# A small first load, one 8 KB run per DMA engine, ahead of a queue of 6 MB loads

## The chip, the cores and the metric

The kernel runs on one core of a Trainium2 chip. The metric is device time of one execution in microseconds (us), median of several runs; lower is better. "Before" and "after" are the two kernels of the change. The profiled run of before took 335.77 us for a span of 334.0 us: the span starts at the program's first instruction on the core, and the time is some 1.8 us longer than the span.

## The reference

Adaptive max pooling of a float32 tensor of 32 x 256 x 4096 down to 256 outputs per row. As 4096 / 256 = 16, it is the maximum of each run of 16 neighbouring elements:

```python
for i in range(output_size):                      # 256
    start = int(i * length / output_size)         # 16 * i
    end = int((i + 1) * length / output_size)
    result[:, :, i] = np.max(x[:, :, start:end], axis=-1)
```

134.2 MB go in, 8.4 MB go out, and every input element is read once.

## The kernel before

The output is seen as 2,097,152 windows in a row. Two groups of windows are dealt to the 128 partitions (rows) of the on-chip memory, 7600 and 8784 windows each. A load brings 760 windows (48,640 B) to every partition, 6080 KB in all; the ring has three slots, so load n waits for the reduction of load n-3. VectorE reduces each slot into an output tile that stays on the chip, and the three stores stand at the end of the same queue.

```python
    SLOTS = 3
    CHUNK = 760
    GROUPS = [10 * CHUNK, total - 10 * CHUNK]     # total = 16384
    CUT = 10 * CHUNK
    ...
    for g, n in enumerate(GROUPS):
        xg = xw[first : first + P * n].rearrange("(p n) w -> p (n w)", p=P)
        ...
        for a in range(0, n, CHUNK):
            b = min(a + CHUNK, n)
            slot = ring[:, n_loads % SLOTS, 0 : (b - a) * W]
            n_loads += 1
            nc.sync.dma_start(out=slot, in_=xg[:, a * W : b * W])
            nc.vector.reduce_max(
                out=outs[g][:, a:b],
                in_=slot.rearrange("p (n w) -> p n w", w=W),
                axis=mybir.AxisListType.X,
            )
        ...                                        # note the stores of the group
    for dst, src in stores:
        nc.sync.dma_start(out=dst, in_=src)
```

That makes 22 loads (21 of 760 windows, a last one of 424) and 3 stores, 25 DMAs on one queue.

## Time and profile before

335.86 us, median of 6 runs (335.66 to 336.07). These are the lines of the page of before: the span, busy time, the slices (40 equal ones, DMA in tenths of the engines' time), the queue and the costliest group (busy us, mean ns of one, idle time before it and what ended it).

```profile
span 334.0 us, 111 instructions
DVE 276.3 (83%) x22; POOL 0.2 (0%) x4
DMA  9999899999999999999998999999999999989997
q1 hardware_dynamic: 3600, 142.61, 99.1%
L59 DVE TENSOR_REDUCE out<-ring 128x760 f32<-128x12160 f32 (+1 forms) x22 | 276.3, 12565 | 49.2 <-DMA ring<-in_x_dram 49.2
```

The DMA engines work all the time (99.1% of the span); VectorE waits only for loads. The timeline of before at its start (start us, us, engine and line, operation) shows the pace:

```profile
0.73 59.20 SPq L58 DMA_DIRECT2D ring<-in_x_dram  x6
18.01 12.82 DVE L59 TENSOR_REDUCE out<-ring 128x760 f32<-128x12160 f32 x1 [18.01 <-DMA ring<-in_x_dram]
32.38 12.82 DVE L59 TENSOR_REDUCE out<-ring 128x760 f32<-128x12160 f32 x1 [1.55 <-DMA ring<-in_x_dram]
46.76 12.82 DVE L59 TENSOR_REDUCE out<-ring 128x760 f32<-128x12160 f32 x1 [1.56 <-DMA ring<-in_x_dram]
```

A load every 14.38 us is 433 GB/s, and a reduction is 1.56 us shorter. Only head and tail are left to gain: the first reduction starts at 18.01 us, 3.6 us later than one load lasts.

The head needs a finer view. The trace holds a record of every DMA packet (one row of one load) and of every raise of a DMA's semaphore, the counter that the program waits for: 400 raises for the 25 DMAs of before, 16 each. No record names the engine; the 16 packets that start together are taken to be one of each engine, and so are the 16 raises of a DMA, called completions below. In the table below, and in all like it, times are us after the first load's issue, and they are read from those records. A row of 48,640 B takes 1.80 us in the steady state (1.796 to 1.81); the first ones do not:

```
                         first packets of 16 engines:  start          took          median
before                                                 1.01 to 2.44   1.79 to 3.09  2.53
first load complete on the earliest / mean / latest engine: 16.31 / 16.67 / 17.26
last store complete on the earliest / latest engine: 331.54 / 332.48
```

The spread of 0.95 us between the engines arises in the first row and is still 0.93 us at the end; over all 25 DMAs it is 0.92 to 0.96 us. The rows behind the first take 1.796 to 1.81 us on all engines, so none catches up, and the kernel ends with its latest engine.

### The profile page before, as it was taken

The page shows a single profiled execution, that of the slowest core. Times are in us where ns is not written, and L with a number is a line of the kernel's source. Part 1 is how long each engine was busy: PE and PEld are TensorE (multiplying, and loading weights), DVE is VectorE, ACT ScalarE, POOL GpSimd, SP SyncE. Part 2 cuts the span into 40 slices and gives each one's busy share as a digit, 9 for nine tenths or more (in the row PEclk, how much of TensorE's full clock was granted, in tenths as well). Part 3 has the DMA queues.
Part 4 walks back from the last instruction along what each step waited for, and adds up shares of the span by engine and source line. Part 5 has one row for each costly group of instructions (what it writes and reads, how often), then busy time and mean ns, then how long its engine had stood idle before and what let it go on. Part 6 is the DMA issues. An engine that isn't in the chain of part 4 may idle for free.

```text
span 334.0 us, 111 instructions
## 1 busy us (share of the span) xinstructions
DVE 276.3 (83%) x22; POOL 0.2 (0%) x4
## 2 busy tenths in 40 slices
DVE  0088989889898988989898898988989898898990
POOL 0000000000000000000000000000000000000000
DMA  9999899999999999999998999999999999989997
GB/s 361 390 460 454 384 466 437 402 466 437 402 460 425 419 454 408 443 454 396 454 454 384 466 437 402 466 419 419 460 414 431 454 408 443 454 384 440 443 419 306
DMA packets 3600, 142.61 MB, mean 427 GB/s; under 512 B 400, under 2 KB 400, under 8 KB 528
## 3 DMA queue, kind: packets, MB, share of 16 engines
q1 hardware_dynamic: 3600, 142.61, 99.1%
HBM read 134.22 MB, written 8.39 MB: 427 GB/s over the span
## 4 chain that ended last, share of the span: by engine, by line
DMA 68%; DVE 27%; DVEq 2%; SPq 0%; issue 0%
DMA ring<-in_x_dram 68%; DVE out L59 27%; DVEq L102 2%; SPq L58 0%
## 5 line engine op out<-in xcount | busy, mean ns | idle before, releaser
L59 DVE TENSOR_REDUCE out<-ring 128x760 f32<-128x12160 f32 (+1 forms) x22 | 276.3, 12565 | 49.2 <-DMA ring<-in_x_dram 49.2
L88 POOL MEMSET const-bfloat16-1.0<- 128x1 bf16 x1 | 0.1, 101 | 0.0
L88 POOL MEMSET const-uint8-127<- 128x1 uint8 x1 | 0.1, 101 | 0.0
L88 POOL MEMSET const-float32-0.0<- 128x1 f32 x1 | 0.1, 98 | 0.2 <-issue 0.2
L88 POOL MEMSET const-float32-1.0<- 128x1 f32 x1 | 0.1, 98 | 0.0
## 6 DMA issues: line engine op xcount, KB each, us to landing
ring<-in_x_dram SPq DMA_DIRECT2D x21, 6080.0 KB, 30.3
out_dram<-out SPq DMA_DIRECT2D x2, 3800.0 KB, 30.1
ring<-in_x_dram SPq DMA_DIRECT2D x1, 3392.0 KB, 23.9
out_dram<-out SPq DMA_DIRECT2D x1, 592.0 KB, 7.6
```

What stands on the lines that cost most here:

```text
L59: nc.vector.reduce_max(out=outs[g][:, a:b], in_=slot.rearrange("p (n w) -> p n w", w=W), axis=mybir.AxisListType.X,)
L88: nc = _bacc.Bacc("TRN2", target_bir_lowering=False, num_devices=1)
L102: with _tile.TileContext(nc) as tc:
```

## The change

The intent is to let the start of the DMA engines fall on a small load: 16 partitions with 8 KB each, meant as one run for each of the 16 engines, at the head of the queue. The remaining windows are dealt to 128 partitions as before, so the last load shrinks from 424 to 408 windows; the small load has its own reduction and its own store, second among the stores.

```diff
-    GROUPS = [10 * CHUNK, total - 10 * CHUNK]
+    FIRST_P, FIRST = 16, 128
+    rest = (total - FIRST_P * FIRST) // P
+    GROUPS = [10 * CHUNK, rest - 10 * CHUNK]
...
+    xf, of = group(FIRST_P, FIRST)
+    first_out = pool.tile([FIRST_P, FIRST], fp32, tag="first", name="first")
+    slot = next_slot(FIRST_P, FIRST)          # ring[0:16, 0, 0:2048]
+    nc.sync.dma_start(out=slot, in_=xf)
+    pooled(first_out, slot)
...
+    stores.insert(1, (of, first_out))
```

The rest of the diff puts loading, slots and reductions into small helpers and changes nothing that runs.

More of the change, by code (lines that the diff above doesn't have):

```diff
@@ L28 @@
     W = L // O
-    total = B * C * O // P
+    total = B * C * O
     SLOTS = 3
     CHUNK = 760
-    GROUPS = [10 * CHUNK, total - 10 * CHUNK]
+    FIRST_P, FIRST = 16, 128
+    rest = (total - FIRST_P * FIRST) // P
+    GROUPS = [10 * CHUNK, rest - 10 * CHUNK]
     CUT = 10 * CHUNK
-    assert sum(GROUPS) == total and B * C * O % P == 0
     pool = ctx.enter_context(tc.tile_pool(name="pool", bufs=1))
     ring = pool.tile([P, SLOTS, CHUNK * W], fp32, tag="ring", name="ring")
-    outs = [
-        pool.tile([P, n], fp32, tag=f"out{i}", name=f"out{i}")
-        for i, n in enumerate(GROUPS)
-    ]
@@ L44, with group, next_slot @@
     xw = x.flatten_outer_dims().rearrange("r (o w) -> (r o) w", w=W)
     ow = out.flatten_outer_dims().rearrange("r o -> (r o)")
+    taken = 0
+    def group(parts, n):
+        nonlocal taken
+        span = slice(taken, taken + parts * n)
+        taken += parts * n
+        return (
+            xw[span].rearrange("(p n) w -> p (n w)", p=parts),
+            ow[span].rearrange("(p n) -> p n", p=parts),
+        )
+    n_loads = 0
+    def next_slot(parts, n):
+        nonlocal n_loads
+        slot = ring[0:parts, n_loads % SLOTS, 0 : n * W]
+        n_loads += 1
+        return slot
@@ new lines, in pooled, with load @@
+    def pooled(dst, src):
+        nc.vector.reduce_max(
+            out=dst,
+            in_=src.rearrange("p (n w) -> p n w", w=W),
+            axis=mybir.AxisListType.X,
+        )
+    def load(dst, src, a, b):
+        slot = next_slot(P, b - a)
+        nc.sync.dma_start(out=slot, in_=src[:, a * W : b * W])
+        pooled(dst[:, a:b], slot)
+    xf, of = group(FIRST_P, FIRST)
+    first_out = pool.tile([FIRST_P, FIRST], fp32, tag="first", name="first")
+    slot = next_slot(FIRST_P, FIRST)
@@ L47 @@
+    nc.sync.dma_start(out=slot, in_=xf)
+    pooled(first_out, slot)
     stores = []
-    n_loads = 0
-    first = 0
     for g, n in enumerate(GROUPS):
-        xg = xw[first : first + P * n].rearrange("(p n) w -> p (n w)", p=P)
-        og = ow[first : first + P * n].rearrange("(p n) -> p n", p=P)
-        first += P * n
+        xg, og = group(P, n)
+        o = pool.tile([P, n], fp32, tag=f"out{g}", name=f"out{g}")
         for a in range(0, n, CHUNK):
-            b = min(a + CHUNK, n)
-            slot = ring[:, n_loads % SLOTS, 0 : (b - a) * W]
-            n_loads += 1
-            nc.sync.dma_start(out=slot, in_=xg[:, a * W : b * W])
-            nc.vector.reduce_max(
-                out=outs[g][:, a:b],
-                in_=slot.rearrange("p (n w) -> p n w", w=W),
-                axis=mybir.AxisListType.X,
-            )
-        if g < len(GROUPS) - 1:
-            stores.append((og, outs[g]))
-        else:
-            for a, b in ((0, CUT), (CUT, n)):
-                stores.append((og[:, a:b], outs[g][:, a:b]))
+            load(o, xg, a, min(a + CHUNK, n))
+        for a, b in ((0, CUT), (CUT, n)):
+            if a < b:
+                stores.append((og[:, a:b], o[:, a:b]))
@@ L70 @@
+    assert taken == total
+    stores.insert(1, (of, first_out))
     for dst, src in stores:
```

## The prediction

> **What bounds the kernel now.** The DMA engines, all the way. The page has DMA at 9 tenths in nearly every slice, mean 427 GB/s; VectorE is busy 83%. The chain of waits repeats every three loads, after 43.1 us: one 6080 KB load costs 14.38 us, 433 GB/s.[...] A reduction takes 12.82 us, 1.56 us less than a load, and the queue never runs dry. The three stores run at the same rate behind the last load. Bytes alone, 142.6 MB at 433 GB/s, are 329.4 us of the 334.0 us span. What is left, about 4.6 us, is head and tail.
>
> **The head.** By the trace's records of DMA packets (a 48,640 B row is one packet), the first issue begins at 0.73 us, the first packets start at 1.74 us, and an engine's first packet takes 2.3 to 3.1 us, where every later one takes 1.796 us. The 16 engines end their first packets between 4.13 and 5.08 us: a stagger of 0.95 us. As all engines then run at one rate and none starves, the stagger is kept to the end: the last store's completions are spread over 0.93 us too. The kernel ends with its latest engine.
>
> **What the change does.** It puts a 128 KB load ahead, one 8 KB run for each of 16 engines ([...]no view of this profile names the engine), so that the start latency falls on a small packet and all engines join together. Total bytes are the same: the last load shrinks from 424 to 408 windows, 8 KB less per engine. Three large loads stay outstanding, as before.
>
> **Costs.** One more load completion, about 0.03 us (14.376 less 8 x 1.793)[...]. Together 0.1 us. The added reduction is 2048 elements deep, estimated 12.82 x 2048/12160 = 2.2 us, while VectorE idles until 18 us: free. The added issue on the sync queue, 0.33 to 0.43 us, is hidden: the 8 KB packet needs 0.3 us at rate plus the latency, and the next load's rows should be there by then.
>
> **Gain.** The first read's latency stays. Only the stagger can go[...]. The most to gain is some 0.6 to 0.9 us; I expect about half, 0.45 us, less the 0.1 us of costs.
>
> **Prediction.** 335.5 us, range 334.9 to 336.1. Faster by over 2%: 0.005; within 2%: 0.985; slower: 0.01.
>
> **What would show it.** Packet records: starts of the first large packets and their spread under 0.95 us (right), or unchanged (no gain). The first 760-window reduction then begins at about 18.0 us or less plus the 0.3 us of the 8 KB packet. The period of 14.38 us and the reductions' 12.82 us stay.
>
> **What would make it wrong.** A hole between the small load and the first large one[...]; a small load that meets as much stagger as a large one; a shift of addresses (the second group's rows are now 548 KB apart, not 549 KB) that changes what HBM delivers.

The forecast's sum is before's 335.86 us, less 0.45 us expected of the stagger, plus 0.1 us of costs: 335.5 us. Only the 0.03 us of a completion are worked out from the trace, so the 0.1 us, like the 0.45 us, are estimates. That the small load gives each engine one run is inferred: in the trace of after, 16 packets of 8 KB start 1.03 to 1.21 us after the issue and take 0.49 to 0.52 us.

## The result, and the profile after

After: 335.88 us, median of 6 runs (335.73 to 336.04), against 335.86 us. The ratio is 1.0001, with a 95% interval of 0.9988 to 1.0014. Ratios here are the mean time of one kernel's fast runs over that of the other's of the same rounds, so not quite the ratio of the medians quoted.

The page of after, the same lines as of before:

```profile
span 334.1 us, 115 instructions
DVE 278.4 (83%) x23; POOL 0.2 (0%) x4
DMA  7998998999999999999989989999999999899997
q1 hardware_dynamic: 3664, 142.61, 99.1%
L67 DVE TENSOR_REDUCE out<-ring 128x760 f32<-128x12160 f32 (+1 forms) x22 | 276.1, 12553 | 43.6 <-DMA ring<-in_x_dram 43.6
L67 DVE TENSOR_REDUCE first<-ring 16x128 f32<-16x2048 f32 x1 | 2.3, 2274 | 3.7 <-DMA ring<-in_x_dram 3.7
```

The timeline of after at its start:

```profile
0.73 0.39 SPq L81 DMA_DIRECT2D ring<-in_x_dram  x1
1.18 59.04 SPq L75 DMA_DIRECT2D ring<-in_x_dram  x6
3.66 2.27 DVE L67 TENSOR_REDUCE first<-ring 16x128 f32<-16x2048 f32 x1 [3.66 <-DMA ring<-in_x_dram]
18.28 12.82 DVE L67 TENSOR_REDUCE out<-ring 128x760 f32<-128x12160 f32 x1 [12.34 <-DMA ring<-in_x_dram]
32.66 12.82 DVE L67 TENSOR_REDUCE out<-ring 128x760 f32<-128x12160 f32 x1 [1.56 <-DMA ring<-in_x_dram]
```

The added reduction lies in time in which VectorE has nothing else to do, the period is 14.38 us as before, and the first large load is reduced 0.27 us later. The small load's 8 KB per engine are worth 0.30 us at the steady rate (8192 / 48,640 x 1.793; 1.793 us is the commonest distance from one row's start to the next on an engine), so almost nothing was gained. The records of packets and completions, with a second trace of each kernel (first experiment below):

```
                 first full load, less bytes ahead       last store   sync's drain after
                 earliest  mean    latest    spread      (latest)     the last completion   span
before           16.31     16.67   17.26     0.95        332.48       0.062                 334.00
before, again    16.32     16.66   17.37     1.05        332.58       0.063                 334.11
after            16.69     16.88   17.22     0.53        332.40       0.194                 334.06
after, again     16.59     16.81   17.25     0.67        332.43       0.194                 334.08
```

"Less bytes ahead" means that the 0.30 us of the small load are taken off; "spread" is the latest engine less the earliest; the drain is the instruction of the sync queue behind its last wait. The stagger did shrink, from about 1.0 to 0.6 us. But it shrank because the earliest engines became 0.3 us later; the latest engine, which alone counts, gained less than 0.1 us on average. The last store completes 0.11 us earlier, and the program's end takes 0.13 us longer. Together that is 0.02 us more, the same as the difference of the medians; as one head differs from the next by more than that (before_27 below), so close an agreement is luck.

So there are three questions. Why does the large load behind the small one not start at full rate? Why did the spread shrink all the same? And where do the 0.13 us at the end come from?

### The profile page after: what moved, and what is told of

Same layout as the page of the kernel before. It is cut to its first block, busy times and chain, and to the rows that moved or that the text cites. A ratio compares the mean times of both kernels' runs of the same rounds, so it can differ in the third digit from the quotient of the medians.

```text
span 334.1 us, 115 instructions
## 1 busy us (share of the span) xinstructions
DVE 278.4 (83%) x23; POOL 0.2 (0%) x4
## 3 DMA queue, kind: packets, MB, share of 16 engines
q1 hardware_dynamic: 3664, 142.61, 99.1%
## 4 chain that ended last, share of the span: by engine, by line
DMA 68%; DVE 28%; DVEq 2%; issue 0%
DMA ring<-in_x_dram 68%; DVE out L67 27%; DVEq L128 2%; DVE first L67 1%
## 5 line engine op out<-in xcount | busy, mean ns | idle before, releaser
L67 DVE TENSOR_REDUCE first<-ring 16x128 f32<-16x2048 f32 x1 | 2.3, 2274 | 3.7 <-DMA ring<-in_x_dram 3.7
```

Of the source, the lines that this page charges most:

```text
L67: nc.vector.reduce_max(out=dst, in_=src.rearrange("p (n w) -> p n w", w=W), axis=mybir.AxisListType.X,)
```

## The experiments

Twelve runs were made, two of them repeats and ten of new kernels, on chips 0, 11, 12 and 13. Every ratio is taken against before in the same rounds (its medians were 335.96, 335.85, 335.86 and 335.79 us); the packet tables set traces of different chips side by side. At first there were three theories. **Delivery**: the rows of a 128-row load reach the last engine late, 2.4 us after the issue. **Placement** ("ports" in the texts): a load to 16 neighbouring partitions, as the small one to partitions 0 to 15, takes longer per byte than one to all 128. It was an assumption, to be tested; no view shows a port, and the "4ports" and "16ports" of three labels are names only, for partitions 0 to 15 and for every fourth one from 32 to 92. **First burst**: the first large reads are slow whatever ran before. A fourth came up on the way, **cover**: short rows start cheaply, and enough of them ahead cover the start of the long ones. All four are guesses until a run below shows them.

### before_again and after_again: is the stagger the program's?

Edit: none.

> The kernel before once more, for its packet records: is the head's stagger a property of the program or of one run? All theories of the program: latest completion of the first load again near 17.26 us after the first issue, spread over the engines near 0.95 us, one engine starting some 2.4 us after the issue. If the stagger is chance, spread and latest engine move by several tenths of a us.

> The changed kernel once more. If the head belongs to the program: latest completion of the first large load near 17.52 us after the first issue (0.27 us later than before, of which 0.30 us are the 8 KB ahead), spread near 0.53 us. If it is chance, both move by several tenths.

Measured: 335.89 and 335.86 us (one run each; state unknown, as for any single run), and the lines of the table above. In these two pairs the head belongs to the program, within about 0.1 us (a third trace of before's head, in before_27 below, is 0.3 us off). The late starter does not: no engine of before_again started later than 1.71 us after the issue, while one of before started at 2.44 us.

### split8_step and split8_block: eight loads of 16 rows in place of the first load

```diff
-            nc.sync.dma_start(out=slot, in_=xg[:, a * W : b * W])
+            if n_loads == 1:
+                for j in range(8):
+                    rows = slice(j, P, 8)                # split8_step
+                    rows = slice(16 * j, 16 * j + 16)    # split8_block
+                    nc.sync.dma_start(out=slot[rows], in_=xg[rows, a * W : b * W])
+            else:
+                nc.sync.dma_start(out=slot, in_=xg[:, a * W : b * W])
```

> The kernel before, with its first load cut into eight loads of 16 rows each (rows j, j+8, j+16 ...), so every engine gets one row per load; no small load, no further store. Theory delivery (the rows of a 128-row load reach the last engine only 2.4 us after its issue): every engine has its first row about 1.0 us after the issue, no late starter, latest completion of the first load 0.5 to 1 us earlier than before's 17.26, less 7 x 0.03 us of completions: about 16.7; time about 335.3. Theory first burst (16 large first reads together are slow, whoever issues them): first packets again 2.3 to 3.1 us, latest completion at 17.3 to 17.5, time about 336.1.[...]

> As split8_step, but each of the eight loads takes 16 neighbouring partitions, as the small load of the change does. Theory ports[...]:[...] time up to +43 us, and packets of up to 7 us in the head.[...] Theories delivery and first burst without ports: as split8_step within 0.2 us.

(The +43 us and the 7 us are estimates. Measured were +38.5 us over before and 6.72 us for a load.)

Measured: split8_step 351.14 us (ratio 1.0453, 1.0439 to 1.0467), split8_block 374.42 us (1.1143, 1.1128 to 1.1158). The first reduction, which needs all eight loads, in the timelines of split8_step and of split8_block:

```profile
33.68 12.82 DVE L64 TENSOR_REDUCE out<-ring 128x760 f32<-128x12160 f32 x1 [33.68 <-DMA ring<-in_x_dram]
```

```profile
56.97 12.82 DVE L64 TENSOR_REDUCE out<-ring 128x760 f32<-128x12160 f32 x1 [56.97 <-DMA ring<-in_x_dram]
```

And the GB/s of the slices on the page of split8_block, where the first six slices (9.3 us each) are the eight small loads:

```profile
GB/s 167 84 120 131 84 162 423 418 418 418 433 470 433 418 418 418 470 449 418 418 418 433 470 433 418 418 423 470 444 418 418 418 438 470 428 418 419 438 424 326
```

One 760 KB load over 16 neighbouring partitions took 6.72 us, so 778,240 B / 6.72 us = 116 GB/s; over partitions 8 apart 3.79 us, 205 GB/s; a load over all 128 runs at 433 GB/s. The pages have the DMA engines busy 7 to 9 tenths of those first six slices in split8_block and 8 to 9 tenths of the first four in split8_step, so idle engines are not what limits these loads.

What follows: a load to 16 neighbouring partitions had about a quarter of the rate of a load to all 128 (116 of 433 GB/s). By what mechanism, the traces do not show. An estimate from the 116 GB/s: the small load's 131,072 B take 1.13 us, not the 0.30 us that I had counted. These two kernels cannot tell delivery from first burst, since the slow placement swamps both.

### dead_small_4ports and dead_small_16ports: does the placement eat the gain at 8 KB?

A load that nothing reads is put at the head of the kernel before, into slot 2 of the ring:

```diff
+    dead = ring[0:16, 2, 0:2048]        # dead_small_4ports
+    dead = ring[32:96:4, 2, 0:2048]     # dead_small_16ports
+    nc.sync.dma_start(
+        out=dead, in_=xw[0 : 16 * 2048 // W].rearrange("(p n) w -> p (n w)", p=16)
+    )
```

> The kernel before with one more load at the head, 8 KB into each of partitions 0 to 15, of data that nothing reads: the change's head alone, without its reduction, its store and its shorter last load. Bytes: 0.30 us more than before. All theories: the head of the changed kernel comes back, latest completion of the first large load 17.5 us after the first issue (before: 17.26 and 17.37 in two traces; after: 17.52 and 17.55), engines spread 0.5 to 0.7 us. Time about 336.2.

> The same, into partitions 32, 36, ... 92[...]. Theory ports[...]: latest completion of the first large load falls below that of the 4-port run by 0.3 us or more, to 17.2 or less; time about 335.9. Theories delivery and first burst: within 0.1 us of the 4-port run.

(That loads to every fourth partition are written faster than loads to 16 neighbours was assumed here.)

Measured: 336.25 us (ratio 1.0014, 1.0001 to 1.0026) and 336.80 us (1.0027, 1.0014 to 1.0039).

```
                      first full load, less 0.30      8 KB packets    first 16 rows of 48,640 B
                      earliest  mean   latest spread  took            start         took (median)
dead_small_4ports     16.71     16.87  17.24  0.53    0.52            1.54 to 2.83  2.49
dead_small_16ports    16.83     17.25  18.04  1.21    0.35 to 0.56    1.81 to 2.67  2.50
```

dead_small_4ports reproduces after's head to 0.02 us, so reduction, store and sizes have no part in it. dead_small_16ports was expected to be better by 0.3 us or more if the placement ate the gain, and within 0.1 us otherwise; it is worse by 0.8 us, which no theory had. It is not a clean comparison: its packets started 1.34 us after the issue, not 1.01, and the next issue came 0.63 us after the first instead of 0.44, both seemingly a cost of the strided partitions. But taking off 0.34 us still leaves 17.70. So the placement does not eat the gain at this size. What stands out is the spread: 0.53 us on partitions 0 to 15, 1.21 us on every fourth one.

### dead_row_16ports: a whole row per engine ahead

```diff
-    dead = ring[32:96:4, 2, 0:2048]
+    dead = ring[32:96:4, 2, 0:12160]
```

with the source cut to match.

> [...]a whole row of 48,640 B per engine, 1.79 us of work each. Theory delivery (the last engine's rows of the 128-row load come 2.4 us after its own issue, 2.9 us after the first): every engine is busy with its one row until 3.3 us, so no engine starts the large load late; latest completion of the first large load 18.3 to 18.5, spread 0.3 us or less; time about 337.0, 0.8 us less than its bytes (before + 1.82 = 337.7). Theory first burst (16 large rows at once take 0.5 to 1.3 us longer, and once only): the same delay falls on the dead row and stays, latest completion 19.1 to 19.2, time about 337.7. If the large load meets the burst a second time, more than 19.2.

(The partitions are those of dead_small_16ports, 32 to 92 in steps of four.)

Measured: 337.79 us (ratio 1.0060, 1.0046 to 1.0073); latest completion of the first full load 19.15 us, spread 0.70 us. Eleven engines started their dead row 1.36 to 1.72 us after the issue, five of them at 2.21 to 2.31 us, although only one row per engine had to be delivered. So a late first start is not the delivery of 128 rows, and theory delivery falls. Less its 1.79 us of bytes this load is at 17.36 us, by the number the "first burst" figure; less the 0.34 us of the strided form, which the expectation had not allowed for, it is at 17.02, between the two. It does not settle first burst.

### before_27: is the end's 0.13 us a matter of counting?

```diff
-            stores.append((og, outs[g]))
+            for a, b in ((0, 2560), (2560, 5120), (5120, n)):
+                stores.append((og[:, a:b], outs[g][:, a:b]))
```

> The kernel before with its first store in three parts, 27 DMAs as in the changed kernel, the head untouched. In the traces of after, the sync queue waits at the end for the last store's semaphore first, and three finished ones are still to be waited for: its drain begins 0.194 us after the last completion, against 0.062 us before. If that comes of the count of DMAs alone (eight semaphores in turn), it shows here as well: 0.19 us. Two further completions cost 2 x 0.03 us in the stores. Time about 336.1, 0.2 us over before. If the end's wait comes of the small load or its store: 0.06 us and about 335.95.

Measured: 336.37 us (ratio 1.0013, 1.0001 to 1.0026). The drain begins 0.195 us after the last completion, as in after. The dead-load kernels with 26 DMAs have 0.126 and 0.127 us, before with 25 has 0.062. In the traces of before and after, the DMAs take eight semaphores in turn (48 or 64 raises on each), and the sync queue waits for them at the end in the same order of four pairs, 65 to 70 ns from one wait that is met to the next. With 25 DMAs (before) the last store's semaphore is in the last pair, with 27 (after) in the second (not the first, as the expectation has it), and so, by the turn, with 26 in the third; the later waits follow although they have long been met. So the change's 0.13 us come of having two DMAs more, not of what they do. The two added stores, which also have shorter rows (10,240 B against 30,400), cost 0.15 us between the last load and the last store (19.70 against 19.55 us), more than the 0.06 us expected of two completions. In the profiled run the rest came from the head, which is before's own program: its latest engine was at 17.63 us this time. So the latest engine of before has 17.26, 17.37 and 17.63 us in three traces, and a difference of 0.2 us in the time of one kernel is chance.

### first_256: 16 KB per engine instead of 8 KB

```diff
-    FIRST_P, FIRST = 16, 128
+    FIRST_P, FIRST = 16, 256
```

> The changed kernel with a first run of 16 KB per engine in place of 8 KB (the last load shrinks by as much). [...] Two theories are left for why the large load behind the 8 KB pays its own start. Theory cover (8 KB are gone 0.3 to 0.5 us after they start, before the large load's first reads are answered; a longer run covers more of them): latest completion of the first large load, less the bytes ahead (0.60 us), 17.0 or less, where the changed kernel has 17.22 and 17.25; time about 335.6. Theory first burst (the start of 16 large reads at once costs the same whatever ran before): 17.2 to 17.3, time about 335.85.[...]

(A third outcome: if the small load itself, 2.26 us for 256 KB at the 116 GB/s of split8_block, outlasts the start, the latest completion less the bytes ahead is more than 17.4 us.)

Measured: 336.83 us (ratio 1.0029, 1.0016 to 1.0041). Less 0.60 us of bytes, the first full load completes at 17.82 us on the earliest engine and at 18.01 us on the latest: a spread of 0.19 us, the smallest of all, and every engine late. The 16 KB packets took 0.95 to 1.67 us where the rate gives 0.60. At 116 GB/s 256 KB take 2.26 us, and that is 1.66 us more than was taken off. This is the third outcome: the small load, slow where it is placed, outlasts the start. The timeline of first_256 has the first full load reduced 1.35 us later than before's 18.01:

```profile
19.36 12.82 DVE L67 TENSOR_REDUCE out<-ring 128x760 f32<-128x12160 f32 x1 [9.80 <-DMA ring<-in_x_dram]
```

That the placement slows the small load at 8 KB too is seen in its landing. The pages (KB, us from issue to landing) of after, of cols_first (below; the same bytes over all 128 partitions) and of dead_small_16ports (whose packets start 0.33 us later):

```profile
ring<-in_x_dram SPq DMA_DIRECT2D x1, 128.0 KB, 2.9
```

```profile
ring<-in_x_dram SPq DMA_DIRECT2D x1, 128.0 KB, 2.2
```

```profile
ring<-in_x_dram SPq DMA_DIRECT2D x1, 128.0 KB, 2.4
```

By the records the packets of after end 1.54 to 1.73 us after the issue, and the engines complete only at 2.65 to 2.90. In dead_small_16ports the packets end at 1.71 to 2.08, and the engines complete at 2.05 to 2.37. So the completion comes after the end of the packets' records: 1.1 us on partitions 0 to 15, 0.3 us on every fourth one.

It also answers the second question. With the small load on partitions 0 to 15 the spread goes from 1.0 us (no small load) to 0.53 to 0.67 us (8 KB) and 0.19 us (16 KB); with 8 KB per engine placed otherwise it stays at 1.1 to 1.2 us (dead_small_16ports above, cols_first below). The small load does not let the engines join together by taking up their latency. The reading that fits all of these is that the slow placement holds all engines, and so brings the early ones back to the late ones; no view shows what holds an engine, so this last step is inference.

### cols_first and short_first: the same question with all 128 partitions

Both are the kernel before with the loads cut elsewhere. cols_first loads 16 windows of all 128 partitions first (1 KB rows, the same 128 KB as the change); short_first moves the short load of 424 windows from the end to the head and keeps 25 DMAs.

```diff
+    SHORT = total % CHUNK                                       # short_first: 424
+    GROUPS = [SHORT + 9 * CHUNK, 12 * CHUNK]                    # short_first
...
-        for a in range(0, n, CHUNK):
-            b = min(a + CHUNK, n)
+        cuts = [0] + list(range(16 if g == 0 else CHUNK, n, CHUNK)) + [n]      # cols_first
+        cuts = [0] + list(range(SHORT if g == 0 else CHUNK, n, CHUNK)) + [n]   # short_first
+        for a, b in zip(cuts, cuts[1:]):
```

> The kernel before with 16 windows (1 KB) of all 128 partitions loaded first: the same 128 KB ahead as in the change, but [...]with consecutive partitions, eight packets of 1 KB per engine; no store is added, 26 DMAs. It tells ports apart from the form of the strided loads, whose packets started 1.35 us after the issue and not 1.0. Theory ports: latest completion of the first large load, less 0.30, 17.0 or less. No port effect at this size: 17.2 to 17.3, as after. Time 335.8 to 336.0.

> The kernel before with its short load of 424 windows (27 KB rows) first and full loads behind it: 25 DMAs, no small load, the same bytes. If the start's loss grows with the size of the first rows, the last store completes 332.2 us or less after the first issue (before: 332.48 and 332.58; after: 332.41 and 332.43), time about 335.5. Theory first burst, the loss being paid once by whatever large rows come first: 332.4 to 332.7, time 335.8 to 336.0.

Measured: cols_first 336.37 us (ratio 1.0009, 0.9996 to 1.0023), its latest engine, less 0.30, at 17.79 us with a spread of 1.14 us. That is outside both outcomes of the expectation (17.0 or less, 17.2 to 17.3), but it is one trace, of the second slowest of five runs that lie between 335.81 and 336.40 us. The first full load is reduced 0.84 us later than before's:

```profile
18.85 12.82 DVE L59 TENSOR_REDUCE out<-ring 128x760 f32<-128x12160 f32 x1 [15.52 <-DMA ring<-in_x_dram]
```

Its 1 KB packets were through quickly (median 0.06 us), and its first 16 long rows took 2.18 to 3.09 us again. So the small load gains nothing over all 128 partitions and in an ordinary form either. That settles what dead_small_16ports had left unclean.

short_first 335.37 us (ratio 0.9985, 0.9972 to 0.9997; runs 335.26 to 335.52 against 335.80 to 336.10 of before), last store at 332.06 us. The timeline of short_first at its start:

```profile
0.73 52.52 SPq L59 DMA_DIRECT2D ring<-in_x_dram  x6
11.31 7.22 DVE L60 TENSOR_REDUCE out<-ring 128x424 f32<-128x6784 f32 x1 [11.31 <-DMA ring<-in_x_dram]
25.70 12.82 DVE L60 TENSOR_REDUCE out<-ring 128x760 f32<-128x12160 f32 x1 [7.17 <-DMA ring<-in_x_dram]
```

Here the long rows come 9.6 us after the issue and take 1.80 us from the first on. "The loss being paid once by whatever large rows come first" had put the last store at 332.4 to 332.7, and fails.

### head_128: short rows, and enough of them

```diff
-    SHORT = total % CHUNK
-    GROUPS = [SHORT + 9 * CHUNK, 12 * CHUNK]
+    SHORT = 128
+    GROUPS = [SHORT + 9 * CHUNK, total - SHORT - 9 * CHUNK]
```

Against short_first; it is 128 windows of all partitions, eight rows of 8 KB per engine, 23 loads and 26 DMAs.

> As short_first, but with 128 windows of all 128 partitions first: eight rows of 8 KB per engine, 2.42 us of work, [...]consecutive partitions; 26 DMAs, so the end's wait is 0.127 us instead of 0.062. Theory cover (short rows start cheaply, and enough of them must follow each other to cover the start of the first long ones; 0.30 us in cols_first was not enough, 7 us in short_first was): latest completion of the first full load, less 2.42, 17.0 or less, where before has 17.26 to 17.63 and short_first stands at 16.90 when 6.34 us for its missing 336 windows are added; last store at 332.1 us or less after the first issue (before 332.48 and 332.58); time about 335.4. If the long rows pay their own start whatever ran before: 17.3 or more, time 335.9 or more. If short_first's gain was a lucky head, between the two.

Measured: 335.28 us (runs 335.18 to 335.31), before 335.79 us (335.66 to 335.91) in the same rounds, ratio 0.9984, 0.9971 to 0.9998. The timeline of head_128 at its start:

```profile
0.73 61.06 SPq L59 DMA_DIRECT2D ring<-in_x_dram  x7
5.48 2.29 DVE L60 TENSOR_REDUCE out<-ring 128x128 f32<-128x2048 f32 x1 [5.48 <-DMA ring<-in_x_dram]
19.84 12.82 DVE L60 TENSOR_REDUCE out<-ring 128x760 f32<-128x12160 f32 x1 [12.08 <-DMA ring<-in_x_dram]
34.23 12.82 DVE L60 TENSOR_REDUCE out<-ring 128x760 f32<-128x12160 f32 x1 [1.56 <-DMA ring<-in_x_dram]
```

The first full load is reduced at 19.84 us, 1.83 us later than before's 18.01, with 2.42 us of bytes ahead of it: 0.59 us gained. The packet records, beside those of the kernels above:

```
                first packets (16 engines)          first 16 rows of 48,640 B     first full load, less bytes ahead
                bytes    took           median      took           median         earliest  mean   latest  spread
before          48,640   1.79 to 3.09   2.53        (the same)                    16.31     16.67  17.26   0.95
after            8,192   0.49 to 0.52   0.51        1.79 to 2.75   2.39           16.69     16.88  17.22   0.53
cols_first       1,024   0.05 to 0.34   0.06        2.18 to 3.09   2.56           16.66     16.99  17.79   1.14
short_first     27,136   1.01 to 2.12   1.55        1.80           1.80           16.27     16.61  16.90   0.63
head_128         8,192   0.31 to 1.08   0.72        1.80 to 1.81   1.80           16.24     16.41  16.67   0.43
```

(For short_first the 336 windows that its first load lacks are added, 6.34 us.) In head_128 none of the first 16 long rows takes longer than 1.81 us. Here the spread falls because the latest engine comes earlier, by 0.6 us, and not the earliest later. From the latest engine of the first full load (last columns) to the last store, before, short_first and head_128 take 315.22, 315.16 and 315.25 us: the whole gain lies in the head. The last store completes at 331.92 us, 0.61 us before the mean of before's two traces, and the 26 DMAs give 0.065 us of that back at the end. It is faster than before in the same rounds; after ran in other rounds and had before's time in them. A gain of 0.5 us is 0.15%, so by the measure of 2% all of these kernels are the same.

## Why the prediction was right, and where it was not

**The bound.** Right. The queue of large loads runs at 433 GB/s in both kernels, with the same period of 14.38 us; its packets fill 99.1% of the engines' span, and reductions, 12.82 us each, are hidden.

**The time.** Right: 335.5 us with a range of 334.9 to 336.1, measured 335.88. But the forecast gain of 0.35 us did not come. The range also held before's own 335.86 us, so the number would have been right with any small gain or none, and says nothing for the mechanism.

**"So that the start latency falls on a small packet and all engines join together".** This step failed. The small packets paid little (0.01 to 0.22 us over their 0.30 us in two traces), and the long rows behind them paid their own start, 2.39 and 2.48 us in the median for 1.80 us. The hole that the prediction feared did not open: the first long rows start at 1.54 us, as the small packets end, though four of the 16 in after start only after 2.0 us. The small packets end 1.3 to 1.7 us after the first issue, and the first long rows then still take 0.6 us too long. cols_first shows the same over all 128 partitions. Only with 2.4 us or more of short rows ahead (head_128, short_first) did the long rows run at full rate from the first one; between 0.30 and 2.42 us nothing was tried over all 128 partitions.

**"Only the stagger can go", a gain of 0.45 us.** The stagger went from 1.0 to 0.6 us, but by holding the early engines. The latest engine gained 0.01 to 0.15 us, by which traces are compared. I read the spread as the thing to be won; what counts is the completion of the latest engine.

**8 KB at the steady rate, 0.3 us.** Mis-sized. The forecast missed that a load to 16 neighbouring partitions does not have the whole rate: 116 GB/s measured in split8_block against 433, so an estimate of 1.13 us. At 8 KB the latest engine was no later for it (17.22 and 17.25 us less the bytes, against 17.26 and 17.37); at 16 KB it cost about 0.7 us.

**Costs of 0.1 us.** The sum was near by luck, its terms were not. The added store cost nothing visible (from the last load to the last store 19.50 us in both traces of after, 19.54 and 19.55 in those of before), and the end wait alone cost 0.13 us, more than the whole sum.

**Shifted addresses.** Rightly a doubt and not a cause: the period of the second group's loads is 14.38 us in both.

Two things stay open. Why a first long row takes 0.5 to 1.3 us longer than a later one, and why single engines are worst, the records do not say. And head_128 and short_first shorten the first rows and lengthen the cover at once; cols_first shows that short rows alone, 0.30 us of them, do not do it, but no run held the amount of work fixed while the size of the rows changed. Nor did any run start long rows late with nothing ahead of them: the slow ones start 1.0 to 3.0 us after the first issue, the full-rate ones of head_128 and short_first at 3.9 us and 9.6 us, so the time since the first issue stays an untested rival to cover.

## What to carry to other kernels

Here one DMA queue bounds the kernel and never starves (99.1% of the engines' span), and a delay at its head stayed to the end (a spread of 0.95 us in the first load, 0.93 us in the last store). Only the latest engine's completion counted: in a kernel bound in the same way compare that, with the bytes ahead taken off, and not the spread. To soften the start of a queue of long rows, try short rows over all 128 partitions first, and enough of them (here 2.4 us of them were enough and 0.3 us were not); a single small run per engine did not help (ratio 1.0001), and 16 neighbouring partitions were a slow place to put it (116 GB/s). Each DMA more was also a completion (about 0.03 us, an estimate: 14.376 us from load to load less 8 x 1.793 us from row to row) and moved the last store's semaphore in the order of the final waits (0.062, 0.127 and 0.195 us for 25, 26 and 27 DMAs).
